# A hybrid decoder step on one core: mixes stored whole and split on return, and a rebuilt first norm

## The chip, the core and the metric

The kernel runs on one core of a Trainium2 chip. The metric is the device time of one execution in microseconds (us). The engines are named as in the profile: PE (TensorE matmuls), PEld (its weight loads), DVE (VectorE), ACT (ScalarE), POOL (GpSimd), SP (SyncE, which issues nearly all DMAs).

## The reference

One inference step of a two-layer trunk, for 272 prompt rows (16 meta tokens and 256 prompt tokens) and 8 sample rows, so N = 280 columns in all. Layer 0 is RWKV-7 time mixing, layer 1 sliding-window attention. The part that the change touches is the beginning of layer 0:

```python
y = xf * lax.rsqrt(jnp.mean(xf * xf, axis=-1, keepdims=True) + RMS_EPS)   # rmsnorm, times the weight
...
xx = prev - xn                                      # token shift
xm = xn[:, :, None, :] + xx[:, :, None, :] * mu     # six mixes: r, k, v, z, w, a
rkvz = jnp.einsum('btpd,pde->btpe', xm[:, :, :4], w_rkvz)
...
kk = k_h * k_k.reshape(hn)
kk = kk / jnp.maximum(jnp.sqrt(jnp.sum(kk * kk, axis=-1, keepdims=True)), 1e-12)
...
y = y.reshape(B, T, WIDTH) * jax.nn.silu(z)
return y @ w_out, ...
```

D_MODEL is 2048 (16 slabs of 128 rows in the kernel's layout), the width 4096 (64 heads of 64). All data are fp32.

## The kernel before

**Layout and products.** Everything stands transposed: channels on the 128 partitions, the 280 rows along the free dimension. A slab is `[128, N]`. Most products are made of three fp32r products: an operand is split into a high part (`split`, a cast to fp32r on ACT) and a low part (a subtraction on DVE), and `mm3` adds hi x hi, hi x lo and lo x hi. Weights come in units of 256 KB (`raw`, 2 slabs by 256 columns, a ring of four) and are split on arrival into `whi` and `wlo` (rings of five). The operand on the other side, a mix, is a set of eight tiles `mhl` of `[128, 2, 2, N]`: high and low part of two slabs each. A product of one column pair takes 16 slabs x 2 columns x 3 products.

**Phase 0.** `phase0` loads x (`xn`), squares it, sums the squares over the partitions by products with a matrix of ones (`ps_ssq`), takes the inverse root (`rsb`: Sqrt on ACT, then reciprocal and one Newton step on DVE), and forms the mixes in groups of two slabs (`raw_part`, tiles `mst`). The first two column pairs of k are multiplied in plain fp32 (`gemm32`, line 236), straight from the mixes as they come; the others with split operands by `gemm`. Six pairs later all of the first group's k and v columns are done. Between them stand the small decay products (`lora1`), the sums of squared keys (`ps_kk`) and the transposes of v (`ps_vt`). `hold` is an instruction of DVE behind which the low parts are issued until the third pair; before, it is the last step of the third k mix. The order of all engines here comes from a list scheduler, apart from the DVE order of the k mixes.

**Mixes through DRAM.** The k, v and z mixes are written to DRAM as split pairs (`md`, 560 KB for two slabs) in phase 0; the r mix stays in SBUF and is written by `keep_r` in the next phase.

**Phase A.** `drive` writes out PE's order by hand: one step of the main product, then whatever the streams have due (`preps`, `scores`, `solve`, `chain`: the chunked recurrence; `decodes`: the sample rows). The products run r (first group), then k, v; v, k, r; r, k, v; z; then the first part of the output product. At each change of operand the next set of eight mix tiles is loaded by `mix_part`, tile by tile as the last product of the old operand lets go of it: seven times from `md`, and once from `gd`, which holds the first gated outputs as split pairs. The order on ACT, DVE and SP comes from the scheduler. After phase A follow the output product, the shared K/V, attention and the last projection, which the change leaves alone.

Of the kernel before, what the change touches and what calls it, by code (L numbers as in the profile page):

```python
# [1 line left out]

# [17 lines left out]
D = 2048  # L20
# [5 lines left out]
N = L + NS  # L26
# [81 lines left out]
class Kernel:  # L108
    def __init__(self, nc, tc, I, O):
        self.nc, self.tc, self.I, self.O = nc, tc, I, O  # L110

        self.raws, self.los = [], []

        self.wx = self.hold = None
        self.plan = []
        self.pools = {}
# [47 lines left out]
    def pe_order(self, engine=mybir.EngineType.PE):  # L164

        return self.tc.manual_schedule(engines={engine})
# [12 lines left out]
    def split(self, hi, lo, src):  # L179

        self.nc.scalar.copy(hi, src)  # L181
        with self.tc.issue_after(self.hold) if self.hold else contextlib.nullcontext():
            return self.nc.vector.tensor_tensor(lo, src, hi.bitcast(F32), op=ALU.subtract)  # L183
# [24 lines left out]
    def gemm(self, w, name, nk, col, x, n=N, ncol=256, per=2):  # L208

        parts = range(0, ncol, 128)  # L210
        ps = [self.bank(self.pm, f"ps_{name}_{col}_{c}") for c in parts]
        out = [p[:min(128, ncol), :n] for p in ps]
        units = self.wunits(w, name, nk, col, ncol, per)

        for two in zip(units, units):
            for c, o in zip(parts, out):
                for k0, wh, wl in two:
                    for k in range(per):
                        xh, xl = x(k0 + k)
                        cs = slice(c, min(c + 128, ncol))  # L220
                        self.mm3(o, wh[:, k, cs], wl[:, k, cs], xh, xl, k0 + k == 0, k0 + k == nk - 1)
        return out

    def gemm32(self, w, name, nk, cols, x):

        self.first = []
        pools = self.pm, self.pm, self.pc, self.pp
        ps = [self.bank(p, f"ps_{name}_{cols[i // 2]}_{i % 2}") for i, p in enumerate(pools)]
        for k0 in range(0, nk, 2):
            for c, col in enumerate(cols):  # L230
                raw = self.ph.tile([128, 512], F32, tag="raw0", bufs=8, name=f"raw_{name}_{col}_{k0}").rearrange(
                    "p (k c) -> p k c", k=2)
                self.first.append(self.nc.sync.dma_start(raw.rearrange("p k c -> p (k c)"), w[col // 256, k0 // 2]))
                for k in range(2):
                    for i in range(2):
                        self.nc.tensor.matmul(ps[2 * c + i][:, :N], raw[:, k, 128 * i:128 * i + 128], x(k0 + k),
                                              start=k0 + k == 0, stop=k0 + k == nk - 1)
        return [p[:, :N] for p in ps]
# [49 lines left out]
    def phase0(self):  # L288
        nc, I, O, ph = self.nc, self.I, self.O, self.ph
        dma, late = nc.sync.dma_start, nc.scalar.dma_start  # L290
# [8 lines left out]
        ones = ph.tile([128, 128], F32, name="ones0")  # L299
        nc.vector.memset(ones, 1.0)  # L300
        warm = ph.tile([128, 1], F32, name="warm")
        nc.scalar.activation(warm, self.epst, AF.Sqrt)
        sq = dx = ph.tile([128, KT, N], F32, name="dx")
        V, A, MU, AD = nc.vector, nc.scalar, ALU.mult, ALU.add
# [3 lines left out]
        asq(0, 2)  # L308
        vsq(2, 5)
        asq(5, 8)  # L310
        vsq(8, 10)
        add(0, 5)
        asq(10, 12)
        vsq(14, 16)
        asq(12, 14)
        add(10, 14)
        add(10, 12)
        pss = self.bank(self.pe, "ps_ssq")[:, :N]
        ks = (2, 3, 4, 7, 8, 9, 0, 1, 10, 11)
        for k in ks:  # L320
            nc.tensor.matmul(pss, ones, sq[:, k], start=k == 2, stop=k == 11)
        rsb, v, t = (ph.tile([128, N], F32, name=n) for n in ("rsb", "ms0", "mt0"))
        A.activation(rsb, pss, AF.Sqrt, scale=1.0 / D, bias=self.epst)
        V.tensor_scalar(v, pss, 1.0 / D, EPS, op0=MU, op1=AD)
        V.reciprocal(rsb, rsb)
        V.tensor_tensor(t, rsb, rsb, op=MU)
        V.scalar_tensor_tensor(t, t, -0.5, v, op0=MU, op1=MU)
        V.scalar_tensor_tensor(rsb, t, 1.5, rsb, op0=AD, op1=MU)
# [9 lines left out]
        self.md = [self.dram(f"md{m}", [8, 128, 2, 2, N]) for m in range(4)]  # L338
        mu = lambda m, k: self.par[:, P_MU + 16 * m + k:P_MU + 16 * m + k + 1]
        sub = ALU.subtract  # L340
        def raw_part(m, g):
# [21 lines left out]
            if m == 1 and g == 2:  # L363
                self.mixed = last
            return t

        def part(m, g, tile, t=None):

            if t is None:
                t = raw_part(m, g)  # L370
            hl = tile(f"d{m}_{g}")
            self.split(hl[:, 0], hl[:, 1], t)
            if 0 < m < 4:
                dma(self.md[m][g], hl.bitcast(F32))
            return hl
        turn = lambda nm: ph.tile([128, 2, 2, N], F32R, tag="zhl", bufs=2, name=f"zhl{nm}")
# [30 lines left out]
        with self.pe_order(mybir.EngineType.DVE):  # L407
            tk = [raw_part(1, g) for g in range(8)]
        self.hold = self.mixed.ins
        for _ in params:  # L410
            pass
        xr, lora = [], lora1()
        first = self.gemm32(I['a_w_rkvz'][0, 1], "k", KT, (0, 256), lambda k: tk[k // 2][:, k % 2])
# [21 lines left out]
        self.key_norms(0)  # L435
        for p0, todo in ((0, [(4, 0), *run(3, 0, 1), (4, 0), *run(3, 2, 3), (4, 0), (3, 4)]),
# [3 lines left out]
            mixes(todo)  # L440
        self.xr = xr
# [14 lines left out]
    def proj(self, m, x, pairs, dst, gemm=None):  # L456

        nc = self.nc
        for p0 in pairs:
            b, sl = p0 // 4, slice(p0 % 4, p0 % 4 + 2)  # L460
            t = self.sp.tile([128, 2, N], F32, tag="st", name=f"st{m}_{p0}")
            if m == 2:
                vk = self.sp.tile([128, 2, 384], F32, tag="vk", bufs=1, name=f"vk{p0}").rearrange("p a (b c d) -> p (a b c d)", b=3, c=2).rearrange("p (i q j d) -> p i q j d", i=3, q=2, j=2)
            pss = (gemm or self.gemm)(self.I['a_w_rkvz'][0, m], "rkvz"[m], KT, p0 * 128, x)
            for j, ps in enumerate(pss):
                nc.scalar.copy(t[:, j], ps)
                if m == 1:
                    sq = self.ph.tile([128, N], F32, tag="sqp0", bufs=2, name=f"sqp{p0}_{j}")
                    nc.scalar.activation(sq, ps, AF.Square, scale=self.pcol(P_KK, p0 + j))
                    if j == 0:  # L470
                        pk = self.bank(self.py, f"ps_kk{p0}")
                    nc.tensor.matmul(pk[:, :N], self.sel[j], sq, start=j == 0, stop=j == 1)
                if m == 2:
                    pt = self.bank(self.pe, name=f"ps_vt{p0}_{j}")
                    for i, r in enumerate((128, 128, 16)):
                        nc.tensor.transpose(pt[:r, i * 128:i * 128 + 128], t[:, j, i * 128:i * 128 + r],
                                            self.ident)
                    nc.scalar.copy(vk[:, 0:2, :, j], pt[:, 0:256].rearrange("t (i q d) -> t i q d", i=2, q=2))
                    nc.scalar.copy(vk[:16, 2, :, j], pt[:16, 256:384].rearrange("t (q d) -> t q d", q=2))
            nc.sync.dma_start(dst[b][:, sl], t)  # L480
            if m == 1:
                ks = self.ph.tile([128, N], F32, tag="ks0", name=f"ks{p0}")[:4]
                nc.vector.tensor_scalar(ks, pk[:4, :N], 1e-24, None, op0=ALU.max)
                nc.sync.dma_start(self.kr[p0 // 8][2 * p0 % 16:2 * p0 % 16 + 4], ks)
            if m == 2:
                self.store_vt(p0, vk)
# [22 lines left out]
    def scratch(self):  # L509
# [4 lines left out]
        self.gd = [self.dram(f"gd{i}", [128, 2, 2, N]) for i in range(4 * G1 // 2)]  # L514
# [6 lines left out]
    def phase_a(self):  # L521
# [24 lines left out]
        self.drive(self.products(), [self.epilogues(), self.main(), preps, self.decodes(), self.late_gates(), self.keep_r()],  # L546
# [52 lines left out]

    def keep_r(self):  # L600

        for g in range(8):
            yield 10 if g else 4
            self.nc.sync.dma_start(self.md[0][g], self.xr[g].bitcast(F32))
# [104 lines left out]
    def mix_part(self, d, m, h, i):  # L709
        t = self.mix_tile(f"m{m}_{i}_{h}")  # L710
        self.nc.sync.dma_start(t.bitcast(F32), d[h])
# [22 lines left out]
    def end(self, P):  # L734
# [7 lines left out]
        if m == 3 and 'y' in P:  # L742
# [1133 lines left out]
```

## Time and profile before

| | |
|---|---|
| median of 3 runs | 2197.99 us (2196.36 to 2199.01) |
| the profiled execution | 2193.88 us, of which the span from the first to the last instruction is 2191.9 us |
| busy | PE 2108.4, PEld 2006.2, DVE 1710.9, ACT 1275.3, POOL 86.9 us |
| moved by DMA | 453.10 MB, 207 GB/s over the span |
| mean granted PE clock | 0.986 |

A row of a list of instructions gives start, duration, engine, line of the source, operation, output and inputs by the program's names, shapes and count; in brackets the idle time of the engine before it and what ended it. A row that begins with a stretch `a:b` gives its length, the busy time and count of PE, PEld, DVE, ACT and POOL, then the granted clock, the busy share of the DMA engines and GB/s. A row with `<-` between two engines is a sum of waits: total us, times, longest.

### The profile page before, as it was taken

Reading aid. Unit: us, or ns where it says so; the run is one execution under the profiler, and the core shown is the slowest. Engines: PE = TensorE matmul, PEld = TensorE weight load, DVE = VectorE, ACT = ScalarE, POOL = GpSimd, SP = SyncE. Lnnn points to the kernel's source line nnn. Section 1 sums busy time; section 2 is a strip of 40 time slices with the busy share of each in tenths; the row PEclk is TensorE's granted clock in tenths of the full one; section 3 lists DMA queues with packets and bytes.
Section 4 is the critical chain, followed back from the end, with each engine's and each line's share of the span. In section 5 each row is a group of like instructions: output and inputs, shape, how many; then the busy total and the mean of one; then the engine's idle time right before and its main releaser. Section 6 shows DMA issues by size and latency. Waiting matters only on the chain.

```text
span 2191.9 us, 56040 instructions
## 1 busy us (share of the span) xinstructions
PE 2108.4 (96%) x21528; PEld 2006.2 (92%) x21528; DVE 1710.9 (78%) x4118; ACT 1275.3 (58%) x2914; POOL 86.9 (4%) x100
## 2 busy tenths in 40 slices
PE   6998999999999998999999999999999999999997
PEld 5998999999889887998889989999999999999997
DVE  6866767787777776878888786997888888888885
ACT  2557766576766666766666544565555555554443
POOL 0010000000010000000100000110000000000000
PEclk9999999999999999999999999999999999999999
DMA  7887667757666766776645877767554544577774
GB/s 259 301 300 236 191 208 241 209 176 255 202 178 196 242 216 186 260 213 189 195 141 164 275 238 228 241 209 212 155 157 139 166 143 138 170 210 239 231 225 136
DMA packets 277300, 453.10 MB, mean 207 GB/s; under 512 B 53336, under 2 KB 99096, under 8 KB 276640
## 3 DMA queue, kind: packets, MB, share of 16 engines
q1 hardware_dynamic: 276456, 447.44, 66.0%
q8 instruction: 169, 2.77, 0.5%
q10 hardware_dynamic: 576, 2.08, 0.2%
q14 instruction: 99, 0.81, 0.1%
HBM read 385.10 MB, written 68.44 MB: 207 GB/s over the span
## 4 chain that ended last, share of the span: by engine, by line
PE 65%; DMA 5%; DVE 5%; ACT 2%; issue 2%; POOL 1%; SPq 0%; DVEq 0%; POOLq 0%; ACTq 0%
PE ps_z L204 6%; PE ps_z L205 5%; PE ps_z L206 5%; PE ps_ob L206 3%; PE ps_ob L205 3%; PE ps_ob L204 3%; PE ps_q L206 3%; PE ps_q L204 3%; PE ps_q L205 3%; PE ps_oa L205 2%; PE ps_oa L204 2%; PE ps_oa L206 2%; PE ps_r L204 1%; PE ps_o L204 1%; PE ps_k L204 1%
## 5 line engine op out<-in xcount | busy, mean ns | idle before, releaser
L204 PE MATMUL ps_z<-mhlm,whi_z 128*128 128x280 f32 x512 | 160.4, 313 | 0.0
L206 PE MATMUL ps_z<-mhlm,wlo_z 128*128 128x280 f32 x512 | 151.8, 296 | 0.7 <-DVE wlo_z L183 0.7
L204 PE MATMUL ps_q<-bmh,whi_qb 128*128 128x264 f32 x512 | 150.5, 294 | 1.8 <-ACT whi_qb L181 1.8
L205 PE MATMUL ps_z<-mhlm,whi_z 128*128 128x280 f32 x512 | 151.6, 296 | 0.1
L204 PE MATMUL ps_z<-bmh,whi_zb 128*128 128x264 f32 x512 | 147.5, 288 | 0.0
L206 PE MATMUL ps_q<-bmh,wlo_qb 128*128 128x264 f32 x512 | 146.4, 286 | 0.7 <-DVE wlo_qb L183 0.7
L205 PE MATMUL ps_q<-bml,whi_qb 128*128 128x264 f32 x512 | 146.1, 285 | 0.0
L205 PE MATMUL ps_z<-bml,whi_zb 128*128 128x264 f32 x512 | 145.4, 284 | 0.0
L206 PE MATMUL ps_z<-bmh,wlo_zb 128*128 128x264 f32 x512 | 145.4, 284 | 0.0
L204 PE MATMUL ps_ob<-ghi,whi_ob 128*128 128x264 f32 x512 | 145.2, 284 | 0.0
L206 PE MATMUL ps_ob<-ghi,wlo_ob 128*128 128x264 f32 x512 | 144.8, 285 | 0.0
L205 PE MATMUL ps_ob<-glo,whi_ob 128*128 128x264 f32 x512 | 144.5, 283 | 0.0
L181 ACT CAST whi_ob<-raw_ob 128x512 fp32r<-128x512 f32 x128 | 79.2, 621 | 97.0 <-PE ps_ob L205 78.7
L183 DVE TENSOR_TENSOR wlo_r<-raw_r,whi_r 128x512 fp32r<-128x512 f32 x128 | 87.2, 685 | 57.9 <-ACT whi_r L181 56.0
L181 ACT CAST whi_oa<-raw_oa 128x512 fp32r<-128x512 f32 x128 | 79.0, 620 | 91.3 <-PE ps_oa L205 30.5
L183 DVE TENSOR_TENSOR wlo_v<-raw_v,whi_v 128x512 fp32r<-128x512 f32 x128 | 88.0, 691 | 47.7 <-ACT whi_v L181 46.4
L204 PE MATMUL ps_k<-mhlm,whi_k 128*128 128x280 f32 x384 | 120.2, 313 | 2.1 <-ACT whi_k L181 2.1
L204 PE MATMUL ps_v<-mhlm,whi_v 128*128 128x280 f32 x384 | 120.3, 313 | 0.0
L183 DVE TENSOR_TENSOR wlo_k<-raw_k,whi_k 128x512 fp32r<-128x512 f32 x112 | 75.3, 685 | 53.3 <-ACT whi_k L181 49.9
L183 DVE TENSOR_TENSOR wlo_oa<-raw_oa,whi_oa 128x512 fp32r<-128x512 f32 x128 | 87.2, 688 | 36.7 <-ACT whi_oa L181 34.0
L181 ACT CAST whi_zb<-raw_zb 128x512 fp32r<-128x512 f32 x128 | 78.3, 620 | 62.4 <-PE ps_z L205 42.0
L206 PE MATMUL ps_k<-mhlm,wlo_k 128*128 128x280 f32 x384 | 112.6, 293 | 0.3 <-DVE wlo_k L183 0.2
(463 smaller groups left out, 7699.9 us busy)
## 6 DMA issues: line engine op xcount, KB each, us to landing
raw_k<-a_w_rkvz SPq DMA_DIRECT2D x128, 256.0 KB
raw_v<-a_w_rkvz SPq DMA_DIRECT2D x128, 256.0 KB
raw_r<-a_w_rkvz SPq DMA_DIRECT2D x128, 256.0 KB
raw_z<-a_w_rkvz SPq DMA_DIRECT2D x128, 256.0 KB
raw_oa<-a_w_out SPq DMA_DIRECT2D x128, 256.0 KB
raw_qb<-b_w_qz SPq DMA_DIRECT2D x128, 256.0 KB
raw_zb<-b_w_qz SPq DMA_DIRECT2D x128, 256.0 KB
raw_ob<-b_w_o SPq DMA_DIRECT2D x128, 256.0 KB
```

The lines of the kernel that those rows point to most:

```text
L181: self.nc.scalar.copy(hi, src)
L183: return self.nc.vector.tensor_tensor(lo, src, hi.bitcast(F32), op=ALU.subtract)
L204: mm(ps, wh, xh, start=start, stop=False)
L205: mm(ps, wh, xl, start=False, stop=False)
L206: return mm(ps, wl, xh, start=False, stop=stop)
```

## The change

- x is loaded in five pieces on SP's queue (before: four, on SP's and ACT's in turn). Squares, ones products and root stand in an order written out for PE, DVE and ACT. There are twelve ones products on sums of squares (before: ten).
- Five products of ones with ones, whose result nobody reads, stand ahead of the sums, and seven behind them.
- The inverse root is Ln and Exp on ACT alone, without the Newton step.
- `hold` is the last step of the eighth k mix; the high parts are issued behind the root.
- All mixes, r too, are written to DRAM whole (280 KB for two slabs) as soon as they are formed; the z mix is no longer split in phase 0; `keep_r` goes. The first gated outputs go to `gd` whole and are not split before. `mix_part` loads a tile whole and splits it.
- The sums of squared keys and the transposes of v are put off: `gemm` issues them behind the first products of a following pair (`behind`).
- The products of the third and fourth k pair are issued behind the last fp32 product (`lead`); the parameter loads move behind the fp32 product's weight loads.

```diff
     def split(self, hi, lo, src):
-        self.nc.scalar.copy(hi, src)
+        with self.tc.issue_after(self.root) if self.hold else contextlib.nullcontext():
+            self.nc.scalar.copy(hi, src)
...
     def gemm(self, w, name, nk, col, x, n=N, ncol=256, per=2):
...
-                        self.mm3(o, wh[:, k, cs], wl[:, k, cs], xh, xl, k0 + k == 0, k0 + k == nk - 1)
+                        last = self.mm3(o, wh[:, k, cs], wl[:, k, cs], xh, xl, k0 + k == 0, k0 + k == nk - 1)
+            if self.behind:
+                with self.tc.issue_after(last.ins):
+                    self.behind.pop(0)()
...
     def phase0(self):
-        chunks = [(0, 5), (5, 10), (10, 14), (14, 16)]
-        for i, (a, b) in enumerate(chunks):
-            (late if i % 2 else dma)(xz[:, a:b], I['xT'][:, a:b])
+        for a, b in ((0, 4), (4, 8), (8, 12), (12, 14), (14, 16)):
+            dma(xz[:, a:b], I['xT'][:, a:b])
...
+        with self.pe_order(eng.PE, eng.DVE, eng.Activation):
+            filling(5)
+            asq(0, 2)
+            vsq(2, 4)
+            add(0, 2)
+            summed(0, 1)
+            asq(4, 6)
+            vsq(6, 8)
+            add(4, 6)
+            summed(4, 5)
+            asq(8, 10)
+            vsq(10, 12)
+            summed(8, 9, 10, 11)
+            asq(12, 13)
+            vsq(13, 14)
+            summed(12, 13)
+            asq(14, 15)
+            vsq(15, 16)
+            summed(14, 15)
+            A.activation(rsb, pss[:, :N], AF.Ln, scale=1.0 / D, bias=self.epst)
+            self.root = A.activation(rsb, rsb, AF.Exp, scale=-0.5).ins
+            filling(7)
...
-            if m == 1 and g == 2:
+            if m == 1 and g == 7:
                 self.mixed = last
...
+            dma(self.md[m][g], t)
             hl = tile(f"d{m}_{g}")
             self.split(hl[:, 0], hl[:, 1], t)
-            if 0 < m < 4:
-                dma(self.md[m][g], hl.bitcast(F32))
...
-                        part(m, g, turn)
+                        dma(self.md[m][g], raw_part(m, g))
...
-            self.proj(1, x(xk), [p0], self.kd)
+            with self.tc.issue_after(self.lead):
+                self.proj(1, x(xk), [p0], self.kd)
...
     def proj(self, m, x, pairs, dst, gemm=None):
...
             if m == 1:
-                ks = self.ph.tile([128, N], F32, tag="ks0", name=f"ks{p0}")[:4]
...
+                self.behind.append(functools.partial(self.squares, p0, sqs))
             if m == 2:
-                self.store_vt(p0, vk)
+                self.behind += [functools.partial(self.turn_v, p0, j, t, vk) for j in range(2)]
...
     def mix_part(self, d, m, h, i):
         t = self.mix_tile(f"m{m}_{i}_{h}")
-        self.nc.sync.dma_start(t.bitcast(F32), d[h])
+        whole = t[:, 1].bitcast(F32)
+        self.nc.sync.dma_start(whole, d[h])
+        self.split(t[:, 0], t[:, 1], whole)
         return t
...
     def end(self, P):
-            hi, lo = y[:, :, :N].bitcast(F32R), t.bitcast(F32R)
-            self.split(hi, lo, t)
-            for i, a in enumerate((hi, lo)):
-                dma(self.gd[p0 // 2][:, i], a.bitcast(F32))
+            dma(self.gd[p0 // 2], t)
```

More of the change, by code (lines that the diff above doesn't have):

```diff
@@ L161, in close, with pe_order @@
             self.pools.pop(n).__exit__(None, None, None)
-    def pe_order(self, engine=mybir.EngineType.PE):
-        return self.tc.manual_schedule(engines={engine})
+    def pe_order(self, *engines):
+        return self.tc.manual_schedule(engines=set(engines or (mybir.EngineType.PE,)))
     def bank(self, pool, name):
@@ L307, in phase0, with filling, summed @@
         add = lambda a, b: V.tensor_tensor(sq[:, a:a + 2], sq[:, a:a + 2], sq[:, b:b + 2], op=AD)
[L308 to L328, printed above, removed]
+        pss, junk = (self.bank(self.pe, n) for n in ("ps_ssq", "ps_fill"))
+        rsb = ph.tile([128, N], F32, name="rsb")
+        def filling(n):
+            for _ in range(n):
+                nc.tensor.matmul(junk[:, :N], ones, fill, start=True, stop=True)
+        def summed(*ks):
+            for k in ks:
+                nc.tensor.matmul(pss[:, :N], ones, sq[:, k], start=k == 0, stop=k == KT - 1)
+        eng = mybir.EngineType
+        with self.pe_order(eng.PE, eng.DVE, eng.Activation):
[20 more added lines that the diff above has]
+            filling(7)
         mv = [ph.tile([128, 2, 2, N], F32R, name=f"mv{g}") for g in range(8)]
@@ new lines, in squares, with turn_v @@
+    def squares(self, p0, sqs):
+        nc = self.nc
+        pk = self.bank(self.py, f"ps_kk{p0}")
+        for j in range(2):
+            nc.tensor.matmul(pk[:, :N], self.sel[j], sqs[j], start=j == 0, stop=j == 1)
+        ks = self.ph.tile([128, N], F32, tag="ks0", name=f"ks{p0}")[:4]
+        nc.vector.tensor_scalar(ks, pk[:4, :N], 1e-24, None, op0=ALU.max)
+        nc.sync.dma_start(self.kr[p0 // 8][2 * p0 % 16:2 * p0 % 16 + 4], ks)
+        if p0 == 6:
+            self.key_norms(0)
+    def turn_v(self, p0, j, t, vk):
+        nc = self.nc
+        pt = self.bank(self.pe, name=f"ps_vt{p0}_{j}")
+        for i, r in enumerate((128, 128, 16)):
+            nc.tensor.transpose(pt[:r, i * 128:i * 128 + 128], t[:, j, i * 128:i * 128 + r], self.ident)
+        nc.scalar.copy(vk[:, 0:2, :, j], pt[:, 0:256].rearrange("t (i q d) -> t i q d", i=2, q=2))
+        nc.scalar.copy(vk[:16, 2, :, j], pt[:16, 256:384].rearrange("t (q d) -> t q d", q=2))
+        if j:
+            self.store_vt(p0, vk)
```

57 lines of the change are left out of this document (23 added, 34 removed).

## The prediction

> **What bounds the kernel now.** I read the busy totals first, then stretches of the span, then the first 40 us instruction by instruction, because the change rebuilds the start.
>
> ```profile
> span 2191.9 us, 56040 instructions
> PE 2108.4 (96%) x21528; PEld 2006.2 (92%) x21528; DVE 1710.9 (78%) x4118; ACT 1275.3 (58%) x2914; POOL 86.9 (4%) x100
> ```
> ```profile
> 0.00:25.00 25.00, 7.70 (x20) 5.51 (x20) 9.71 (x19) 6.74 (x11) 2.62 (x8) 0.98 0.77 270
> 60.00:150.00 90.00, 90.00 (x631) 84.28 (x631) 76.04 (x156) 53.11 (x105) 6.04 (x10) 1.00 0.92 318
> 150.00:1320.00 1170.00, 1122.50 (x13704) 1051.39 (x13703) 889.91 (x1993) 751.30 (x1771) 47.11 (x47) 0.98 0.68 211
> ```
>
> The columns are window and length, then PE, weight loads, DVE, ACT and POOL busy with counts, granted clock, DMA share, GB/s. TensorE is the bound: in 60 to 150 us it is busy all of 90.00 us although DMA stands at 0.92 and DVE at 76 of 90. The large loss is the first 25 us, with 7.70 us of PE work. The scan phase (150 to 1320) loses 47.5 us in small pieces. So what brings the first projection forward is worth its full length, as long as nothing behind it runs short.
>
> The start, engine by engine:
>
> ```profile
> 7.50 0.74 DVE L306 TENSOR_TENSOR dx<-xn 128x560 f32<-128x560 f32 x1 [6.45 <-DMA xn<-xT]
> 9.76 1.69 DVE L306 TENSOR_TENSOR dx<-xn 128x560 f32<-128x560 f32 x2 [1.52 <-DMA xn<-xT]
> 11.37 2.28 DVE L307 TENSOR_TENSOR dx<-dx 128x560 f32<-128x560 f32 x3
> ```
> ```profile
> 23.52 0.51 DVE L345 SCALAR_TENSOR_TENSOR xn<-xn,par,rsb 128x280 f32<-128x280 f32 x1
> ```
> ```profile
> 11.51 7.70 PE L321 MATMUL ps_ssq<-dx,ones 128*128 128x280 f32 x20 [11.51 <-DVE dx L306]
> 25.25 6.71 PE L236 MATMUL ps_k<-mst,raw_k 128*128 128x280 f32 x16 [6.04 <-DVE mst L354]
> 31.60 0.50 PE L204 MATMUL ps_k<-mhld,whi_k 128*128 128x280 f32 x1
> 31.93 7.71 PE L236 MATMUL ps_k<-mst,raw_k 128*128 128x280 f32 x32
> ```
>
> Squares run 7.50 to 13.65, ones products 11.51 to 19.21, the root and first mix until 25.25. Each fp32 product is two recorded instructions.
>
> ```profile
> 25.30:30.50 5.20, 5.20 (x11) 3.82 (x12) 0.50 0.00 0
> 32.00:39.00 7.00, 7.00 (x30) 5.64 (x30) 1.00 0.67 217
> ```
>
> After its 6.04 us of idling PE gets a granted clock of 0.50 for 5.2 us: 11 instructions in 5.20 us (0.47 each) against 30 in 7.00 (0.233). Later PE never idles; behind 25.25 us it is fed.
>
> **Part by part.** *x and the squares.* The loads become five pieces on SP alone, of 4, 4, 4, 2 and 2 slabs, instead of 5, 5, 4, 2 on two queues.
>
> ```profile
> 0.00:3.00 3.00, 0.00 (x0) 0.00 (x0) 0.24 (x4) 1.31 (x2) 0.41 (x5) 1.00 0.44 77
> 3.00:4.50 1.50, 0.00 (x0) 0.00 (x0) 0.00 (x0) 0.17 (x1) 0.00 (x0) 1.00 0.95 374
> 4.50:6.00 1.50, 0.00 (x0) 0.00 (x0) 0.00 (x0) 0.00 (x0) 0.00 (x0) 1.00 0.98 410
> 6.00:7.50 1.50, 0.00 (x0) 0.00 (x0) 0.00 (x1) 0.00 (x1) 0.00 (x0) 1.00 1.00 406
> ```
> ```profile
> xn<-xT SPq DMA_DIRECT2D x1, 722.5 KB
> ```
>
> The last row's 722.5 KB are five slabs, so a slab is 0.148 MB and the first ten 1.48 MB. The rates give 0.23 MB moved by 3.0 us, 0.79 by 4.5, 1.41 by 6.0, so 1.48 MB at 6.2; their reader started at 7.50, thus 1.3 us after the last byte. In one queue's order four slabs (0.59 MB) pass at 4.0, eight at 5.4, all sixteen (2.37 MB) at about 8.4: released at 5.3, 6.7 and 9.7 (now the last at 9.76). Square 0.74 and add 2.28/3 = 0.76 put the first ones product at 6.8 instead of 11.51. There are now twelve products, 24 instructions at 0.24 = 5.8 us, plus 0.6 waiting for the second add (6.8 after the first, + 0.74 + 0.76 = 8.3), so 13.2. Five filling products (ten instructions at 0.47 = 4.7 us) run ahead, a little less than the 5.2 us that the slow clock lasted; I add 0.6 and take 13.8. The bounds: 12.6 with no gap at full clock; 16.5 if the first piece is released only at 7.50 (first product at 9.0) and seven instructions still run at 0.47. Against 19.21: **-5.4** (-6.6 to -2.7).
>
> *Root.* Ln and Exp stand in the trace once, in the later norm:
>
> ```profile
> 1452.04 0.50 ACT L1375 ACTIVATE rb<-ps_sta,epst 128x280 f32<-128x280 f32 x1 [0.26 <-PE ps_sta L1373]
> 1452.43 3.88 ACT L1383 ACTIVATE bmh<-hT,par 128x280 fp32r<-128x280 f32 x9
> 1456.33 1.28 ACT L1376 ACT_TABLE_LOAD   x1
> 1457.62 0.44 ACT L1376 ACTIVATE rb<-rb 128x280 f32<-128x280 f32 x1
> ```
>
> Exp had its own table load although Ln had run just before, and I expect it again; the warm-up Ln covers only the first. Ln 0.50 + load 1.28 + Exp 0.44 = 2.2, the unchanged DVE steps to the first mix 25.25 - 23.52 = 1.73, hand-overs 0.2 (an estimate): 4.1 against 6.04, **-1.9** (-3.2 without the load, -1.0 if hand-overs cost 1 us more). The Trainium skill, "ScalarE: Activation LUTs", section "Table sets: the hidden batching unit", says that Ln and Exp share one set, so that only one load is paid. The trace disagrees with its 1.28 us load ahead of Exp; by the page this term would be -3.2 and the whole sum 1.3 us better.
>
> *Filling and clock.* Seven more filling products take 14 x 0.24 = 3.4 us from 13.8, to 17.2; the first k product is ready at 13.8 + 4.1 = 17.9, so they delay nothing and leave no long idle. The 0.50 clock over 5.2 us cost 2.6 us of work: **-2.6** (-2.9 to 0, zero if the clock drops anyhow). The Trainium skill, "TensorE: Matmul & The Clock Gate", Part 1, says that about 3.4 us of sustained work end the half clock. Here it lasted 5.2 us, longer than the page has it; by the page the 0.6 us added above would go.
>
> *k mixes.* The scaling that opens the second and the third group of two slabs:
>
> ```profile
> 26.71 0.93 DVE L345 SCALAR_TENSOR_TENSOR xn<-xn,par,rsb 128x280 f32<-128x280 f32 x2
> ...
> 29.36 0.93 DVE L345 SCALAR_TENSOR_TENSOR xn<-xn,par,rsb 128x280 f32<-128x280 f32 x2
> ```
>
> A DVE group lasts 29.36 - 26.71 = 2.65 us; PE needs 16 x 0.24 = 3.84. The second group is ready 2 x 1.6 + 2.65 = 5.9 us after the root, PE asks at 1.73 + 3.84 = 5.6: **+0.4** (0 to +1). Later `hold` moves to the eighth group, so the fp32r low parts of eight k mixes and five weight tiles queue on DVE behind it: 13 x 0.7 = 9.3 us, between the end of the mixes (root at 16.1 + 21.8 = 38) and that of the fp32 product (17.9 + 0.4 + 30.7 = 49). They fit; without that gap up to 9 us would show. Eight weight loads (2.1 MB, some 5 us at 400 GB/s) land by about 15, ahead of 17.9.
>
> *At nothing.* Key squares and V transposes are put behind the next weights. The largest PE wait between 26 and 205 us after the first product belongs to the decay path, not to these:
>
> ```profile
> PE ps_l L204 <- ACT cl L819: 2.9, 2, 2.2
> ```
>
> PE had other products to run there, which is the cover; without it they would still find their data ready. The parameter loads move behind 16 weight loads on SP, and POOL's three scalings with them; their first users come after the fp32 product. Halved stores meet a full PE in 60 to 150 and gain nothing there.
>
> *Mixes split on return.*
>
> ```profile
> 29.48 0.66 ACT L181 CAST mhld<-mst 128x560 fp32r<-128x560 f32 x1 [2.00 <-DVE mst L361]
> ```
> ```profile
> 36.57 0.73 DVE L183 TENSOR_TENSOR mhld<-mst,mhld 128x560 fp32r<-128x560 f32 x1
> ```
> ```profile
> mhlm<-md SPq DMA_DIRECT2D x56, 560.0 KB
> ```
> ```profile
> L204 PE MATMUL ps_k<-mhlm,whi_k x81: 287/292/500, 288.0 to 340.0; 128*128 128x280 f32 x81
> ...
> L711 SPq DMA_DIRECT2D mhlm<-md x8: 319/326/377, 270.7 to 288.2; - x8
> ```
>
> The 56 loads, and eight of the gated outputs, shrink to 280 KB and each gains a cast and a subtraction: 64 x 0.66 = 42 us of ACT, 64 x 0.73 = 47 us of DVE, less eight of each that the z outputs lose. The loads are issued 17 us ahead of use (270.7 against 288.0), which covers landing and split. Not covered is the queue: weight casts wait behind a cast whose load has not landed, and weight loads wait on the subtractions:
>
> ```profile
> SPq L197 <- DVE wlo_z L183: 79.3, 52, 4.8
> ```
> ```profile
> 628.00:738.00 110.00, 106.14 (x1393) 98.81 (x1392) 88.34 (x193) 72.48 (x175) 8.13 (x6) 1.00 0.60 176
> 738.00:782.00 44.00, 41.51 (x411) 37.85 (x410) 33.03 (x74) 30.05 (x75) 5.26 (x4) 1.00 0.81 260
> 809.00:854.00 45.00, 42.43 (x542) 38.71 (x540) 32.83 (x89) 24.74 (x54) 0.00 (x0) 1.00 0.81 255
> ```
> ```profile
> 821.84 9.01 DMA raw_v<-a_w_rkvz
> ```
>
> Two change-overs idle PE 2.5 us each, the quiet stretch 3.9 in 110 (3.5%). One more split per half adds 8 x 0.73 = 6 us to DVE's 33 of 44 (75 to 88%), at a price I estimate at 0.5 us per change-over, as if one of the eight subtractions of 0.73 us stood mostly in the way: +4 for eight. Against it, 2.3 MB less per change-over should shorten landings like raw_v's 9.01 us and win back 0.5 of the 2.5 us: -4. Net **0** (-8 to +19, both worked out below).
>
> Sum: -5.4 - 1.9 - 2.6 + 0.4 = **-9.5 us**. The profiled execution took 2193.88 us (2191.9 span and 2.0 around it), so 2184.4. It lies 4.1 under the median 2197.99 of the runs shown; on that scale I forecast 2188.5.
>
> **Rivals.** *DMA relief pays.* The change-overs idle PE 2.5 us, the chain runs through the 9.01 us weight load, and DMA is at 0.81 against 0.60. If halved traffic brings them to 1.5 us each, eight save 8 us: 2180.5. Against it: 3.5% of idling in the quiet stretch without such traffic.
>
> *Splits block ACT (slower).*
>
> ```profile
> ACT sm L868 <- DMA vT<-vd: 20.5, 8, 3.3
> ```
>
> ACT already stops in order for freshly issued loads, 2.6 us each time here. In 738 to 782 it has 14 us to spare; eight casts of 0.66 use 5.3, so it overflows from a stop of (14 - 5.3)/8 = 1.1 us each, and then weight casts run late. At 1.4 us it is 0.3 x 8 x 8 = 19 us: 2207.5. It takes 1.25 us to eat the gain of the start. Against it: the 17 us of lead.
>
> *Half of the start.* The first piece is released at 7.50 and the clock stays low: -2.7 - 1.9 - 0.5 + 0.4 = -4.7, 2193.3.
>
> *Start eaten.* The 13 held low parts come late, up to 9.3 us: 2197.8. DVE at 76 of 90 speaks for it, the free 11 us against.
>
> **How the numbers follow.** Forecast 0.45, relief 0.20, blocked ACT 0.13, half start 0.12, eaten 0.10. The forecast's own bounds are 2183 to 2195; the range 2177 to 2202 takes in relief with 3 us more, the eaten start, and only the mild end of blocked ACT. A measurement can tell about 0.2% (4.4 us): faster means below 2193.6, slower above 2202.4. Faster is 0.42 of the forecast, all relief, 0.07 of the half start, 0.02 of the eaten one: 0.71; slower the blocked ACT, 0.13; the rest 0.16.
>
> **What would show it.** Right: ones products end near 14, one table load between Ln and Exp, first k product near 18 at full clock, the fp32 product done near 49, and the first r product 9 to 10 us before its old place, with later landmarks keeping that lead. Wrong: a lead under 5 us at 60 us (start), a PE gap near 49 (held parts), or a lead that shrinks or grows at each change-over, with ACT waiting on mhlm loads or the weight landings shortened. My sum fails if the lead at 1320 us differs from that at 150 by over 5 us.

## The result, and the profile after

The changed kernel takes 2211.41 us (median of 13 runs, 2203.01 to 2222.26), the kernel before, run beside it, 2199.01 us (13 runs, 2193.71 to 2205.4). The ratio is 1.005 (95% interval 1.0033 to 1.0068): slower, where 2188.5 us and "faster" were forecast, and outside the range of 2177 to 2202. (The expectations below write 1.0055 for it, nearly the quotient of the two medians.) The profiled execution took 2212.53 us.

The totals of the page of the changed kernel:

```profile
span 2210.7 us, 56246 instructions
PE 2122.0 (96%) x21556; PEld 2015.4 (91%) x21556; DVE 1739.7 (79%) x4163; ACT 1299.6 (59%) x2964; POOL 88.8 (4%) x100
DMA packets 275269, 423.29 MB, mean 191 GB/s; under 512 B 53224, under 2 KB 96936, under 8 KB 274608
```

And the same three stretches as in the prediction:

```profile
0.00:25.00 25.00, 21.92 (x80) 16.34 (x81) 13.74 (x34) 10.74 (x17) 1.21 (x8) 1.00 0.82 292
60.00:150.00 90.00, 90.00 (x644) 84.94 (x643) 69.54 (x142) 44.77 (x94) 6.04 (x10) 1.00 0.75 238
150.00:1320.00 1170.00, 1109.41 (x13537) 1036.31 (x13535) 910.25 (x2024) 769.18 (x1804) 50.39 (x47) 0.98 0.62 186
```

The first row shows 21.92 us of PE work where there were 7.70: the start is gained. The last row shows the loss. In the same 1170 us PE now works 1109.41 us where it worked 1122.50, and gets through 13537 instructions instead of 13704, although the DMA engines carry less (0.62 against 0.68).

The start, engine by engine (timelines of PE and ACT):

```profile
6.84 1.21 PE L324 MATMUL ps_ssq<-dx,ones 128*128 128x280 f32 x4 [0.67 <-DVE dx L314]
8.34 4.99 PE L324 MATMUL ps_ssq<-dx,ones 128*128 128x280 f32 x20 [0.29 <-DVE dx L314]
13.17 3.46 PE L320 MATMUL ps_fill<-fill,ones 128*128 128x280 f32 x14
17.38 30.51 PE L242 MATMUL ps_k<-mst,raw_k 128*128 128x280 f32 x128 [0.75 <-DVE mst L374]
```
```profile
13.37 0.49 ACT L346 ACTIVATE rsb<-ps_ssq,epst 128x280 f32<-128x280 f32 x1 [3.29 <-PE ps_ssq L324]
13.88 1.28 ACT L347 ACT_TABLE_LOAD   x1
15.17 0.44 ACT L347 ACTIVATE rsb<-rsb 128x280 f32<-128x280 f32 x1
```

All of this came as forecast: the first ones product at 6.84 (6.8), their end at 13.33 (13.8), one table load of 1.28 us between Ln and Exp, the first k product at 17.38 (18), and 128 fp32 instructions in 30.51 us without a gap. The first r product is issued at 142.8 us instead of 153.1.

To see where the lead goes, I take the start of the same PE instruction in both traces, before minus after. The numbers in the first column count the instructions of that product (k or r) from 0. The third column is another profiled execution of the kernel before (run before_again, below), for scale; the last is a kernel that the experiments come to:

| PE instruction | before starts at | before_again | after | late_split |
|---|---|---|---|---|
| first r product | 153.1 | 1.9 | 10.3 | 9.0 |
| k, instruction 479 (behind r to k) | 323.2 | 2.3 | 5.3 | -0.3 |
| r, instruction 863 (behind k to r) | 622.1 | 2.6 | -7.2 | -1.8 |
| first z product | 913.5 | -4.4 | -15.3 | -4.5 |
| last product of the last projection | 2177.5 | -7.4 | -18.5 | -2.2 |

So some 26 us go between 153 and 914 us (19 when set against before_again). This is the stretch in which PE changes from one set of mixes to the next seven times, and nothing is lost afterwards that an ordinary execution does not lose too. The stretch from the first r to the first z product, in before, after and late_split (the rows have the form of those above):

```profile
153.10:913.50 760.40, 732.08 (x8854) 683.95 (x8854) 558.46 (x1252) 502.79 (x1212) 33.42 (x34) 0.99 0.70 213
142.80:928.90 786.10, 746.44 (x8856) 696.36 (x8855) 590.50 (x1300) 530.45 (x1260) 37.17 (x32) 0.97 0.63 187
144.10:918.00 773.90, 740.58 (x8855) 691.87 (x8854) 592.59 (x1302) 530.69 (x1265) 32.96 (x32) 0.98 0.64 191
```

For the same work PE idles 39.7 us instead of 28.3, and its instructions take 14.4 us more, at a lower granted clock: in the records of the clock, stretches of 0.50 add up to 44.4 us, where before has 13.7 and before_again 20.5. So less than half of the loss is idling; the rest is half clock.

What changed there shows in the waits of ACT, 250 to 1320 us, of the changed kernel (total us, times, longest):

```profile
ACT mhlm L184 <- DMA mhlm<-md: 37.4, 23, 5.3
ACT mhlm L184 <- DMA mhlm<-gd: 7.0, 4, 3.1
```

There is no such row before, since ACT had nothing to do with returned mixes. DVE, which subtracts behind the cast, stops with it:

```profile
DVE mhlm L186 <- ACT mhlm L184: 28.6, 23, 4.2
```

What one of these stops does is seen on ACT's and then on PE's timeline:

```profile
816.02 1.39 ACT L184 CAST whi_k<-raw_k 128x512 fp32r<-128x512 f32 x2 [0.68 <-PE ps_k L208]
822.75 1.41 ACT L184 CAST mhlm<-mhlm 128x560 fp32r<-128x560 f32 x2 [5.34 <-DMA mhlm<-md]
824.07 0.62 ACT L184 CAST whi_k<-raw_k 128x512 fp32r<-128x512 f32 x1
824.71 0.26 ACT L896 COPY sr<-ps_sm 96x128 f32<-96x128 f32 x1
...
826.95 0.58 ACT L1085 COPY ET<-ps_so 32x512 f32<-32x512 f32 x1 [0.79 <-DVE ET L1085]
```
```profile
827.58 1.38 PE L1090 MATMUL ps_so<-TT,ET 32*32 32x32 f32 x64 [2.21 <-ACT ET L1085]
```
```profile
828.40:831.80 3.40, 3.40 (x34) 3.10 (x29) 3.40 (x8) 1.18 (x2) 0.00 (x0) 0.50 0.85 273
```

ACT stands 5.34 us before one cast whose tile has not landed. Behind it in its queue wait a weight cast, copies for the sample rows and `ET`, a step of the recurrence. PE, which follows its own written order, reaches the product that needs `ET` and idles 2.21 us. Right behind that the granted clock is 0.50 for 3.4 us (the last row is a stretch of the windows view). A full PE at half clock loses half the time, so the stall of 2.21 us comes to about 3.9 us (an estimate: 2.21 and half of 3.4). At 833.95 us the next such stop on ACT takes 4.05 us, and PE stalls again for a step `W` of ACT (1.65 us at 838.96). It is such steps that PE waits for, and not the weights: between 250 and 1320 us its waits for weight casts, 5.2 us before, are 0.2 us here, and its waits for other work of ACT are 27.5 us against 16.4 (19.8 in before_again).

### The profile page after: what moved, and what is told of

It is laid out like the page before. It is cut to its first block, busy times and chain, and to the rows that moved or that the text cites. A ratio compares the mean times of both kernels' runs of the same rounds, so it can differ in the third digit from the quotient of the medians.

```text
span 2210.7 us, 56246 instructions
## 1 busy us (share of the span) xinstructions
PE 2122.0 (96%) x21556; PEld 2015.4 (91%) x21556; DVE 1739.7 (79%) x4163; ACT 1299.6 (59%) x2964; POOL 88.8 (4%) x100
## 4 chain that ended last, share of the span: by engine, by line
PE 63%; DVE 6%; DMA 5%; ACT 3%; issue 2%; POOL 1%; SPq 0%; DVEq 0%; POOLq 0%; ACTq 0%
PE ps_z L207 5%; PE ps_z L208 4%; PE ps_z L209 4%; PE ps_ob L209 3%; PE ps_ob L208 3%; PE ps_ob L207 3%; PE ps_q L209 3%; PE ps_q L207 3%; PE ps_q L208 3%; PE ps_oa L208 2%; PE ps_oa L207 1%; PE ps_oa L209 1%; DMA mhlm<-md 1%; PE ps_r L207 1%; PE ps_v L207 1%
## 5 line engine op out<-in xcount | busy, mean ns | idle before, releaser
L207 PE MATMUL ps_v<-mhlm,whi_v 128*128 128x280 f32 x384 | 123.0, 320 | 0.1
L207 PE MATMUL ps_k<-mhlm,whi_k 128*128 128x280 f32 x384 | 121.9, 317 | 0.3 <-ACT st L754 0.3
L209 PE MATMUL ps_v<-mhlm,wlo_v 128*128 128x280 f32 x384 | 114.5, 298 | 0.0
L208 PE MATMUL ps_v<-mhlm,whi_v 128*128 128x280 f32 x384 | 114.4, 298 | 0.0
```

What stands on the lines that cost most here:

```text
L207: mm(ps, wh, xh, start=start, stop=False)
L208: mm(ps, wh, xl, start=False, stop=False)
L209: return mm(ps, wl, xh, start=False, stop=stop)
```

## The experiments

All ratios are against the kernel before, run on the same chip beside each kernel, with 95% intervals. The expectations weigh three explanations. Theory A: ACT stops, in order, at casts of mixes that have not landed. Theory B: the work of 64 casts and 64 subtractions is too much. Theory C: the rest of the change, or half clock behind stalls at random places, loses the time.

**The storage alone.** The kernel before, with only the mixes and gated outputs whole in DRAM and split on return (the stores change with it, and `keep_r` goes):

```diff
-        self.nc.sync.dma_start(t.bitcast(F32), d[h])
+        whole = t[:, 1].bitcast(F32)
+        self.nc.sync.dma_start(whole, d[h])
+        self.split(t[:, 0], t[:, 1], whole)
```

> The kernel before with the storage part alone: mixes and gated outputs whole in DRAM, split on return; start, root and the rest as before. Theories A and B: it loses what the changed kernel lost after its first r product, about 28 us: ratio 1.010 to 1.014. Theory C: no loss, 0.998 to 1.002.

Measured: 2219.02 us, 1.0104 (1.0077 to 1.0132). By itself this part costs some 23 us, twice what the whole change costs.

**All but the storage.** The changed kernel with split pairs in DRAM again (`md`, `gd`, `keep_r`):

> The changed kernel with one part undone: mixes and first gated outputs go to DRAM as split pairs again and come back split (560 KB a tile, no split on return, r written by keep_r). The new start stays. In the trace of the changed kernel PE led the kernel before by 10.5 us at the end of the first r product and trailed by 18.5 us at the end, having lost ground at the change-overs. Theory A (ACT stops in order at the casts of mixes that have not landed) and theory B (the 64 casts and 64 subtractions are too much work for ACT and DVE) both expect the lead to stay: about 10 us under the kernel before, ratio 0.995. Theory C (the loss comes from the rest of the change, whose new order shifts phase A's schedule) expects no gain: ratio 1.000 to 1.005.

Measured: 2201.29 us, 1.0022 (1.0004 to 1.004). The loss is not all storage: the new start with the other parts gains nothing at the end. Put beside this kernel, the storage costs the changed kernel only 0.0028, against 0.0104 in the kernel before. Both differences are uncertain by 0.0025 to 0.003, yet they do not agree. I return to this below.

**Waiting without the work.** The pairs kernel, with a one-column copy on ACT of each returned tile: ACT must wait for the landing, but splits nothing.

```diff
         self.nc.sync.dma_start(t.bitcast(F32), d[h])
+        w = self.rp.tile([128, 1], F32, tag="dumw", bufs=2, name=f"dumw_{i}_{h}")
+        self.nc.scalar.copy(w, t[:, 1, 1, N - 1:N].bitcast(F32))
```

> As pairs, but ACT also copies one column of each returned mix tile into scratch (64 small copies), so that it waits for the landing in its order without the work of a split. The tile is still 560 KB, so it lands later than a whole one would. Theory A: most of the 28 us come back, ratio to the kernel before 1.003 to 1.008. Theory B: stays near pairs, 0.995 to 0.997.

Measured: 2213.69 us, 1.007 (1.0048 to 1.0091), so 0.005 over the pairs kernel, for 64 copies of one column. That is some 11 us, not most of the 28 that the expectation speaks of; but DVE does not stop here, and the tiles still have 560 KB. The waits of ACT in this kernel, 250 to 1320 us:

```profile
ACT dumw L745 <- DMA mhlm<-md: 49.5, 40, 4.7
```

**The work without the waiting.** A pairs kernel with the work of the 64 splits on data that is always there (run pairs_work) gave no time: its tiles did not fit into the on-chip memory (125.7 KB per partition, with 121.9 left). So the wait was taken out instead. The changed kernel, each tile's split put off by four tiles, and its cast behind the newest weight cast:

```diff
-        self.split(t[:, 0], t[:, 1], whole)
+        self.unsplit.append(t)
+        if len(self.unsplit) > 4:
+            self.split_one()
         return t
+    def split_one(self):
+        t = self.unsplit.pop(0)
+        with self.tc.issue_after(self.cast):
+            self.split(t[:, 0], t[:, 1], t[:, 1].bitcast(F32))
```

(The last four of a set are split ahead of the column pair that follows.)

> The changed kernel, each returned tile split four tiles later, its cast put behind the newest weight cast on ScalarE. All 64 splits remain. If ScalarE's stops in order at casts of tiles that have not landed are what costs (theory A), the waits of 37.4 us of ACT on mhlm loads fall below 10 us and the ratio to the kernel before falls from 1.0055 to 0.999 to 1.002. If it is the work of the 64 casts and subtractions (theory B), the waits fall but the ratio stays at 1.004 to 1.007. Under theory C (half-clock windows after short stalls land at random), 1.002 to 1.007, with no tie to the waits.

Measured: 2196.3 us, 0.9978 (0.9962 to 0.9994): faster than both kernels, with all 64 splits in it. Its rows of ACT's longest waits hold no mix tile any more. At the place shown above ACT now runs through:

```profile
823.19 0.65 ACT L185 CAST mhlm<-mhlm 128x560 fp32r<-128x560 f32 x1
824.00 0.66 ACT L185 CAST mhlm<-mhlm 128x560 fp32r<-128x560 f32 x1 [0.16 <-DMA mhlm<-md]
827.28 0.66 ACT L185 CAST mhlm<-mhlm 128x560 fp32r<-128x560 f32 x1
```

The same in the kernel before, storage and late splits only:

> The kernel before with whole storage and each returned tile split four tiles late (the old start, everything else old). With the splits at once this storage measured 1.0104. If stops of ScalarE are the whole price of the storage (theory A), ratio 0.999 to 1.002; if halved traffic also pays once they are gone, 0.995 to 0.998 (the step from the pairs kernel at 1.0022 to late_split at 0.9978 would be that relief); if the work of the splits costs (B), 1.004 to 1.008.

Measured: 2203.07 us, 1.0027 (1.0009 to 1.0045). Of the 0.0104 of the storage, 0.0077 are gone. What is left is the work, or something else: 1.0027 lies between the answers for A (up to 1.002) and B (from 1.004), and tells no more. Its trace is a warning, too. ACT's waits for mix tiles are down to 1.2 us there, yet from the first r to the first z product that execution (2209.95 us, among its slowest) takes 781.0 us, as long as the profiled one of the storage alone (2214.73 us, its fastest). The price of the waits is read from the medians; one trace alone does not show it.

**The splits on GpSimd.** The changed kernel with both steps of the split on GpSimd, which is busy 4% of the span:

```diff
-        self.split(t[:, 0], t[:, 1], whole)
+        self.nc.gpsimd.tensor_copy(t[:, 0], whole)
+        self.nc.gpsimd.tensor_tensor(t[:, 1], whole, t[:, 0].bitcast(F32), op=ALU.subtract)
```

> The changed kernel with cast and subtraction of the 64 returned tiles on GpSimd instead of ScalarE and VectorE. ScalarE no longer stops for these landings and both engines lose the work, so theories A and B both expect 0.999 to 1.002 (as the pairs kernel, or better by the halved traffic); with late_split it tells A from B. If GpSimd's two operations take over 4 us a tile, eight take over 32 us, more than the 17 us of lead, and TensorE waits for the parts at the change-overs: 1.01 and more, with PE waits on mhlm.

Measured: 2237.58 us, 1.0177 (1.0154 to 1.0201), the slowest of all, and not for the reason that I had named: the two steps take 0.916 and 1.614 us, 2.5 us a tile, well under 4, and PE waits for them 2.5 us in all. GpSimd is not idle: it forms `nd`, `N` and `Noff` of the recurrence. Its groups and one row of its waits:

```profile
L738 POOL TENSOR_TENSOR mhlm<-mhlm 128x560 fp32r<-128x560 f32 x64 | 102.5, 1614 | 0.3
L737 POOL CAST mhlm<-mhlm 128x560 fp32r<-128x560 f32 x64 | 58.3, 916 | 271.7 <-DMA mhlm<-md 239.6 <-DMA mhlm<-gd 18.9 <-PE ps_k L209 3.8
```
```profile
POOL mhlm L737 <- DMA mhlm<-md: 239.6, 24, 66.6
```

The stop in order has only moved to an engine that meets each cast earlier still, and behind it stand steps of the recurrence, too. That this is the price is read from the trace, not tried. DVE's weight subtractions also grew, from 0.686 to 0.846 us for `wlo_oa`, and the two causes are not told apart.

**The start alone.** The kernel before with the new `phase0` down to the root, nothing else:

> The kernel before with the new start alone (five loads on one queue, squares in set order, twelve products, filling, Ln and Exp); mixes stored and returned as pairs, key squares and V transposes in their old place, hold at the third group. First r product 9 to 10 us earlier in every theory. If the loss of the lead in the pairs kernel comes from what else the change moves (deferred squares and transposes, hold, parameter loads), the lead is kept: ratio 0.995 to 0.997. If the scan phase does not keep an earlier start, whatever moves (theory C), the lead fades between the first r product and 900 us: ratio 1.000 to 1.002.

Measured: 2196.19 us, 0.9986 (0.9968 to 1.0004). The first r product is 10.5 us early, the median gains 3 to 4 us.

**Without the deferral.** The pairs kernel with key squares and V transposes right behind their own projection:

> The pairs kernel (ratio 1.0022) with key squares and V transposes back right behind their own projection. If their deferral delays what the decay path and the first chunk products wait for, ratio 0.995 to 0.998; if the scan phase loses the lead by itself, 1.001 to 1.003 as in the pairs kernel.

Measured: 2197.44 us, 0.9998 (0.9979 to 1.0017), between my two answers. The same edit in the kernel with late splits:

> The changed kernel with late splits and with key squares and V transposes back in their old place. If their deferral costs the 0.0024 between pairs and pairs_inline: 0.994 to 0.997; if that difference was chance: 0.997 to 0.999 as late_split.

Measured: 2198.02 us, 0.9999 (0.9981 to 1.0017): there it costs 0.0021 where it gained 0.0024 in the other. Each difference is about as large as its uncertainty (0.0025). The deferral has no price of its own that these runs can show. And the start together with the late splits:

> The kernel before with the new start and the late splits, nothing else of the change. The start alone measured 0.9986. If the parts add (start -0.0014, late splits about -0.004 of relief): 0.993 to 0.996. If the scan phase gives back what comes earlier (C): 0.997 to 1.000.

Measured: 2196.89 us, 0.999 (0.9974 to 1.0007). The relief that was hoped for is not there. With late splits as they measured in the kernel before (+0.0027) and the start (-0.0014), the sum is 1.0013, so that the parts add within the uncertainty of three measurements.

**How much one execution differs from the next:**

> The kernel before once more, for a second profile of it. If the profiled execution of before was a lucky one, the lead of one execution over another of the same kernel wanders by 4 us or more between 150 and 1350 us, with half-clock windows in other places; if executions repeat, the landmarks agree within 1 us and the lost lead of the new start is due to the kernels.

Measured: 2201.2 us, span 2199.2, 7.3 us over the first profile of the same kernel. The column in the table above shows where: between 622 and 914 us, where this execution has stretches of 0.50 clock that the other lacks. The forecast had been built on an execution on the low side, and had allowed 4.1 us for that.

**Does a shift of the start reach the end?** The kernel before, with 20 copies of the root onto itself on ACT:

```diff
         A.activation(rsb, pss, AF.Sqrt, scale=1.0 / D, bias=self.epst)
+        for _ in range(20):
+            A.copy(rsb, rsb)
```

> The kernel before with 20 ScalarE copies of the root (about 0.44 us each, 8.8 us) between the root and the first mix; every TensorE instruction stays as it was. If the scan phase passes a shift of its start through to the end: ratio 1.003 to 1.005 (8.8 us of 2200). If it takes shifts up (theory C, which would also eat the 10 us of the new start): 1.000 to 1.002.

Measured: 2211.08 us, 1.005 (1.0032 to 1.0067), 11 to 12 us for a first r product 8.0 us late. The scan phase takes up nothing that these runs can show. The kernel with the new start, delayed in the same way by 22 copies:

> The kernel with the new start alone (0.9986) with 22 such copies behind the root, which puts the first r product back to where it was before, 152 to 155 us. If shifts pass through: 1.003 to 1.005 (9.7 us and up to 2.6 us for a clock that drops again). If they are taken up: 0.999 to 1.001. If the new start alone lost its gain to other places of its 28 more TensorE instructions (gaps in which TensorE waits for nothing that the profile shows), these 28 cost 3 to 7 us here too, and this is slower than the kernel before by that.

Measured: 2212.48 us, 1.0054 (1.0036 to 1.0072). Its first r product stands 4.1 us later than in the first profile of before (6.0 against before_again), and its median is 12 us higher (8 to 16 by the interval). Against the new start without copies the first r product moved 14.6 us and the time by 0.0068, 15 us. So theory C is wrong as I had put it: a shift is not absorbed. The new start, as built here, brings a cost of some 6 to 8 us behind it (uncertain by 4).

**The filling products:**

```diff
-            filling(5)
...
-            filling(7)
```

> The kernel with the new start alone (0.9986) without its twelve filling products. The sum gave the clock 2.6 us: the 24 instructions of the twelve ones products and the first k products run at a granted clock of 0.50 in part, first k product 1 to 3 us later than with filling, first r product 2 to 5 us later; ratio 0.999 to 1.001 if that passes through, 0.9986 or less if the gaps of the 28 instructions were the loss (24 of them gone).

Measured: 2192.57 us, 0.9976 (0.9959 to 0.9993), the lowest ratio of all. Filling brings the first r product 4.9 us forward (147.5 against 142.6), yet the kernel without it is no slower. Without filling the start keeps what it gains: its first r product comes 5.6 us before its old place, and its ratio is worth 5 us. The opposite test, 28 filling instructions ahead of the ones products in the kernel before, where they move its start little:

> The kernel before with 14 filling products (28 TensorE instructions, as many as the change adds) ahead of its ones products, where TensorE waits for x. The first k product stays within 2 us of its place. If 28 more instructions ahead cost the 4 to 7 us that start_only and start_slow lose behind the first r product (gaps in which TensorE waits for nothing shown): ratio 1.001 to 1.004. If the loss is not tied to them: 0.999 to 1.0005.

Measured: 2204.15 us, 1.0026 (1.0007 to 1.0044), though its first r product comes 3.2 us early. PE's timelines of start_only, start_slow and before_fill show a stall at one and the same instruction (number 1974, counted from 0 and without the 28 added ones):

```profile
270.08 0.23 PE L1060 MATMUL ps_so<-TR,ET 32*16 32x16 f32 x4 [2.35 <-issue]
```
```profile
286.01 0.23 PE L1062 MATMUL ps_so<-TR,ET 32*16 32x16 f32 x4 [2.02 <-issue]
```
```profile
277.62 0.23 PE L1051 MATMUL ps_so<-TR,ET 32*16 32x16 f32 x4 [1.44 <-issue]
```

"Issue" is idle time in which PE waited for nothing that the profile shows. These three kernels start this instruction at three different times, and each stalls just there, and again at number 11644 (a z product: 1.27, 1.10 and 1.61 us) and number 13427 (an o product: 0.98, 0.71 and 0.70 us). The kernel before in both its profiles, before_slow and start_nofill go through all three places without a stop. These gaps go by the place in PE's stream of instructions, not by the time at which it arrives. Streams without the 28 have such gaps at other instructions of the program, and the place that counts is the one from the very start of the stream: in 13 of the nineteen traces a gap of 0.62 to 1.90 us stands at instruction 10142 to 10144 of all, whether 0, 4 or 28 were added ahead. What 28 more change is thus which product meets them. In total, from 143 to 2180 us, they are 9.8, 7.8 and 6.3 us in the three, and 3.4, 5.2, 8.2 and 5.3 us in the four others. That is too small and too mixed a difference to call it the whole of what the start loses.

Whether filling should go was then tried in the changed kernel and in the best one:

> The changed kernel (1.0055) without its filling products. If filling costs more behind the start than its clock gains (start_only 0.9986 against start_nofill 0.9976): 1.002 to 1.005. If the clock term of 2.6 us holds to the end: 1.006 to 1.008.

Measured: 2219.84 us, 1.0088 (1.0058 to 1.0117).

> The changed kernel with late splits (0.9978) and without filling. If both corrections add: 0.994 to 0.997; if the clock term holds to the end: 0.998 to 1.000.

Measured: 2201.23 us, 1.0008 (0.999 to 1.0026). Both went the other way: there filling is worth 0.003 to 0.004, some 7 to 8 us, though with an uncertainty of 5 to 8 us it cannot be told from the 4.9 us by which it brings the first r product forward. So "28 more instructions cost time" does not hold in general either. What remains open is why one part is worth up to 0.003 more or less in another company. Each edit shifts where stalls fall, and which of them have half clock behind them; that this is the reason is not shown.

## Why the prediction was wrong

- *x and the squares, -5.4*: right. The ones products ended at 13.33 instead of 19.21, -5.9.
- *Root, -1.9*: right. From the end of the ones products to the first k product 4.05 us (4.1 forecast). The Trainium skill, "ScalarE: Activation LUTs", section "Table sets: the hidden batching unit", has Ln and Exp in one set; the 1.28 us load between them is there again, now at the start.
- *Filling and clock, -2.6*: right in size for the k products, but not all that filling does. Without it the first r product comes 4.9 us later in the otherwise same kernel (start_nofill against start_only). Some 2.9 us of it is the half clock of the k products, which lasts until 25.4 us. The other 2.0 us is the ones products: without filling their instructions start 0.47 us apart until 11.7 us (the records of the clock begin only there), as they did in the kernel before until 16.8. So part of the -5.4 hung on filling, too.
- *k mixes, +0.4* (its own figures, 5.9 and 5.6, give 0.3): no wait is seen in the 30.51 us of fp32 products. The held low parts fitted: the next product follows at 47.51 without a gap.
- *"At nothing"*: the deferral moved the pair of kernels on which it was tried once by +0.0024 and once by -0.0021, each within its uncertainty, so zero was a fair size.
- *Splits on return, 0*: this is the step that failed. It was +0.0104 in the kernel before (23 us against my upper end of +19). The reasoning was that loads issued 17 us ahead of use cover landing and split. They do cover PE: between 250 and 1320 us none of its waits is for a mix tile. But the cast stands in ACT's queue close behind the load's issue, not 17 us later, and everything else of ACT stands behind it. In the changed kernel the early casts cost 0.0072 (against late_split), some 16 us of the 23 us between the forecast 2188.5 and the measured 2211.4; against the pairs kernel the storage as a whole shows only 0.0028, 6 us. What is left is the start's lead that did not last, below.
- *The rival "Splits block ACT"* had the stop and the place. Its size, 2207.5, is partly luck: it took 64 stops of 1.4 us, over a threshold of 1.1 us, and had weight casts run late. The trace has 27 stops of (37.4 + 7.0) / 27 = 1.6 us, which by the rival's own slack (0.7 us for each of the 64 casts) would not have overflowed, and PE waited for steps of the recurrence and not for weights. I gave it 0.13 and cited "the 17 us of lead" against it, which is no argument about an engine that waits at the other end of that lead.
- *"As long as nothing behind runs short"*: the lead at 1320 us against that at 150 was the test that the prediction set itself, and it failed by 27 us (20 against before_again). The sum had no term for what a stall drags behind it at half clock. Without the storage the lead does not last either (pairs, 1.0022, where the forecast of -9.5 us alone makes 0.9957); which wait takes it there stays open.
- *DMA relief, -4*: not seen apart. With late splits, whole storage against pairs is +0.0027, -0.0044, +0.0004 and +0.0001 in four companies (before_late against before, late_split against pairs, late_start against start_only, late_inline against pairs_inline); the mean is -0.0003, each uncertain by some 0.0025. On average halved traffic and 64 splits come out even, as the forecast's net had it, once nothing stands in line for a landing.

## What to carry to other kernels

When a transfer gets a consumer on a busy engine, ask when that engine reaches the consumer in its queue, not when the last user needs the data: the margin is landing minus arrival there. If the engine would come first, keep the load early and issue the consumer late, behind work that is due anyway; here that turned 1.005 into 0.9978. And compare a change of 10 us in 2200 with more than one profiled execution of the kernel before, since two of them differed by 7.3 us.

## What the runs showed of the hardware

- Short stalls are followed by half clock. Counted on PE's timelines between 150 and 2180 us, PE has 24 and 26 stalls over 0.9 us in the two profiles of before and 37 in the changed kernel. There each of the eight over 2.0 us has a 0.50 stretch that begins within 2.3 us of its end and lasts 3.4 us or a multiple of that. In all nineteen traces, a 0.50 stretch begins in the stall or up to 3.4 us behind it, or runs already, at all 26 stalls of 3 us or more, at 104 of 127 of 2 to 3 us, and at 152 of 419 of 0.9 to 2 us. The Trainium skill, "TensorE: Matmul & The Clock Gate", section "Why this matters for your kernels", warns of gaps over about 3 us; here 2 us were mostly enough, and now and then 1 us, while one of 2.97 us in the first profile of before brought none.
- PE can idle 0.6 to 3.4 us for no wait that the profile shows, at places that go by the count of its instructions: 13 of nineteen traces have such a gap at instruction 10142 to 10144 from the start, though what stands there differs by up to 28 instructions. What happens there stays open.
- On GpSimd the subtraction of 128x560 took 1.614 us (pool_split), on DVE 0.745 (the changed kernel).
